# A third score buffer, four score banks and a vector-matrix product in half rows, in the recurrence of a two-block model

## The chip, the cores and the metric

The kernel runs on one core of a Trainium2 chip as one launch. The metric is device time in microseconds (us) of that launch; the time shown for a version is a median over runs. The engines are named as the profile names them: PE (TensorE, matrix products), PEld (its weight loads), DVE (VectorE), ACT (ScalarE), POOL (GpSimd), SP (SyncE, which issues most DMAs).

## The reference, cut to what matters

Two blocks act on 512 positions of width 1024. The first one mixes with a gated recurrence in two directions over 256 context and 512 sequence positions, 8 heads of 64, and is modulated by six vectors that come from a vector-matrix product:

```python
mod = jax.nn.silu(c) @ ada_w[l] + ada_b[l]            # 1024 -> 6 * 1024
sh1, sc1, g1, sh2, sc2, g2 = jnp.split(mod, 6)
...
def step(S, inp):                                     # one position of the recurrence
    r_t, w_t, kk_t, b_t, v_t, k_t = inp
    sa = jnp.einsum("bhvk,bhk->bhv", S, kk_t)
    S = S * w_t - sa * b_t + v_t * k_t                # (axes left out)
    return S, jnp.einsum("bhvk,bhk->bhv", S, r_t)
...
x = x + g1 * out_x                                    # then a gated conv FFN with sh2, sc2, g2
```

The first third of `mod` (sh1, sc1) is needed before the recurrence. The other two thirds (g1, sh2, sc2, g2) are needed only after it: "the second part of the modulation" of this text. Block two (another mixer, an FFN) follows and is not touched.

## The kernel before, in words

**Stages.** The recurrence is worked in chunks of 64 positions: 4 context chunks, 8 sequence chunks, in both directions (d = 0 and 1). The 8 heads are taken two at a time, which gives four stages, j = 0 to 3, written by `stage`. A stage has 12 steps g, each for both directions. A step solves for its chunk with a precomputed 64x64 inverse and updates the state `S0`:

- `pr` = A V + KR S0, copied by ACT to `R`; `pu` = XT R, copied by ACT to `U` with a minus; `p3` = kt0 V + S0 + kt1 U, copied by ACT to `S0` with a scale; in the 8 sequence chunks also `py` = three products, copied by ACT to `Y`.

Each product is one call of `mmh`, two 64x64 matmuls for the two heads of the pair. The trace calls the PSUM tiles of all of them `c`, R and U together `RU`, and S0 `S`; the lists of the instruction order give the tiles numbers.

**Scores and keys.** Every second step `pair` makes the inputs of two chunks for each direction: the scores `psc` (PE), which DVE copies through a mask into `AS` (L730), and the transposed keys `pkt` (PE), which ACT copies to `kbt` (L188). `AS` has two buffers for each direction and `psc`, `pkt`, `pv`, `pg`, `py` share two PSUM banks (tag `sc`). Four more banks hold the steps: `C1[d]` for pr, pu and py, `C2[d]` for p3. The last two of the eight belong to the preparation.

**Preparation.** `prep(j)` computes what stage j needs: decays, keys, and by `inverse` the matrices `XT`. It begins on DVE with a transpose `U<-AK` (L662), goes on with 31 pairs of dependent DVE operations (`tmp<-U,X`, L670, and `X<-X,tmp`, L671), then two transposes `F<-X` (L673, L674), matmuls `pt` (L690) and `po`, and ACT copies into `XT` (for stage 1 the trace calls it `zx`). `AK` has one buffer, so the inverse of j + 1 begins only after the `pt` matmuls of j have read it. Preparation 1 begins before the recurrence; 2 and 3 run beside stages 0 and 1 and into 2.

**The second part of the modulation.** `ada12` (L525 on) makes 32 output columns of 128: for each, a DMA of 512 KB into a buffer `w`, and one DVE multiply with a running sum (L540) of 128x1024 elements by silu(c). It takes part in the work list only from stage 2 on, because its buffers come from a pool that opens after preparation 3.

**After the stages.** `gn(j)` normalises the output of stage j over 12 small steps beside stage j + 1; for j = 3 there is no later stage, and beside it run the first products of the output projection, `px` (L169 to L171), on inputs 0 to 6, which `rwkv` emits behind the loop, and the splits of its weights on ACT and DVE (`whi` L181, `wlo` L182). The last input, `ahi[7]`/`alo[7]`, comes out of `gn(3)`; behind it `out_proj1` begins (L910).

**What sets the order.** The Python code only emits instructions with a priority number; a scheduler builds one fixed queue for each engine from data dependences, priorities and a model of durations. Each engine then works its queue strictly in order: an instruction that waits holds up everything behind it. Step g of a stage has priority base + 200 g; `gn` 300 later, preparation about 110 later (`PG`, `PF`, `PK`).

Of the kernel before, what the change touches and what calls it, by code (L numbers as in the profile page):

```python
# [122 lines left out]
class K:  # L123
# [8 lines left out]
    PK, PG, PF = 200, 300, (110, 105, 118, 0)  # L132
# [393 lines left out]
    def ada12(self):  # L526

        nc, wp = self.nc, self.wp
        tags = [("w", self.wbufs), ("whi", self.wsbufs), ("wlo", self.wsbufs)]
        cb, sb = (wp.tile([P, 1024], F32, tag=tags[i][0], name="cb", bufs=tags[i][1]) for i in (1, 2))  # L530
        nc.sync.dma_start(out=cb, in_=self.A["cb"])
        nc.scalar.activation(out=sb, in_=cb, func=AF.Tanh, scale=0.5)
        nc.vector.tensor_scalar(out=sb, in0=sb, scalar1=0.5, scalar2=0.5, op0=ALU.mult, op1=ALU.add)
        nc.vector.tensor_tensor(out=cb, in0=sb, in1=cb, op=ALU.mult)
        acc = wp.tile([P, 32], F32, name="adacc")
        for n in range(32):
            yield
            w, t = (wp.tile([P, 1024], F32, tag=tags[i][0], name="adaw", bufs=tags[i][1]) for i in (0, 2))
            nc.sync.dma_start(out=w, in_=self.A["adat"][n])
            nc.vector.scalar_tensor_tensor(out=t, in0=w, scalar=1.0, in1=cb, op0=ALU.mult, op1=ALU.mult, accum_out=acc[:, n:n + 1])  # L540
            if n in (7, 23, 31):
                a = 0 if n == 7 else 8 if n == 23 else 24
                nc.vector.tensor_tensor(out=self.mod[:, 16 + a:17 + n, 0], in0=acc[:, a:n + 1], in1=self.v("ada_b", 16 + a, n + 1 - a), op=ALU.add)
# [91 lines left out]
    def mmh(self, out, lt, rt, start=True, stop=True):  # L635

        for h in range(2):
            hs = slice(64 * h, 64 * h + 64)
            self.nc.tensor.matmul(out[hs], lt[hs], rt[hs], start=start, stop=stop)
# [63 lines left out]
    def stage(self, j, S, todo, rb, gn):  # L703
# [10 lines left out]
        def pair(i, d):  # L714
# [19 lines left out]
            kt = r2.tile([P, 2, 2, 64], F32, tag="kbt", name="kbt", bufs=4)  # L734
# [4 lines left out]
        for g in range(12):  # L739
            at = base + self.PK * g  # L740
            with self.prio(at):
                if g % 2 == 0:
                    for d in range(2):
                        pair(g // 2, d)
                for d in range(2):
                    c = chunk(d, g)
                    A, kt, KR, x = cells.pop((d, c))
                    V, S0 = vt[:, c, :], self.S0[d]
                    R, U = (self.RU[d][g % 2][:, i, :] for i in range(2))
                    pr, pu, py = (self.C1[d][:, i * 64:i * 64 + 64] for i in range(3))  # L750
                    p3 = self.C2[d][:, 0:64]
                    self.mmh(pr, A[:, 0:64], V, True, g == 0)
                    if g:
                        self.mmh(pr, KR[:, 0:64], S0, False, True)
                    nc.scalar.activation(out=R, in_=pr, func=AF.Copy)
                    if g < 11:
                        self.mmh(p3, kt[:, 0], V, True, False)
                        if g:
                            self.mmh(p3, id2, S0, False, False)
                    self.mmh(pu, XT[:, 12 * d + c, :], R)  # L760
                    nc.scalar.activation(out=U, in_=pu, func=AF.Copy, scale=-1.0)
                    if x:
                        self.mmh(py, A[:, 64:P], V, True, False)
                        self.mmh(py, KR[:, 64:P], S0, False, False)
                    if g < 11:
                        self.mmh(p3, kt[:, 1], U, False, True)
                        nc.scalar.activation(out=S0, in_=p3, func=AF.Copy, scale=S["PC"][d][:, c:c + 1])
                    if x:
                        self.mmh(py, A[:, P:192], U, False, True)
# [9 lines left out]
    def gn(self, j, Y, bo, vt):  # L779
# [8 lines left out]
        pv = self.ps2.tile([P, 8, 64], F32, tag="sc", name="pv", bufs=2)  # L788
# [7 lines left out]
        def gate():  # L796
            pg = self.ps2.tile([P, NX], F32, tag="sc", name="pg", bufs=2)
# [26 lines left out]
        py = self.ps2.tile([P, 8, 64], F32, tag="sc", name="py", bufs=2)  # L824
# [569 lines left out]
```

## Time and profile before

| | |
|---|---|
| median of 3 runs (1590.5 to 1594.64) | 1591.91 us |
| the profiled execution: its own time, and its span | 1588.74 us, 1586.9 us |
| busy: PE | 1503.9 us (95%) |
| busy: DVE | 1000.5 us (63%) |
| busy: ACT | 631.3 us (40%) |
| busy: POOL | 124.0 us (8%) |
| the L540 multiplies | 32, 1235 ns each |
| the DMAs of `adaw` from `in_adat` | 32 of 512 KB, median 4.5 us to landing |

A page of the profile gives each engine's busy time. Small matmuls are pipelined, so a PE that counts as 90% busy in the recurrence can be one that mostly waits for ACT between two products: what bounds that stretch is read from the order of time and from the waits, not from the share.

### The profile page before, as it was taken

What the parts mean: (1) busy time and instruction counts of PE and PEld (TensorE: products, weight loads), DVE (VectorE), ACT (ScalarE), POOL (GpSimd) and SP (SyncE); (2) the same over time, 40 slices, a digit from 0 to 9 for tenths busy, and PEclk for the clock granted to TensorE, in tenths of its full rate; (3) what the DMA queues carried; (4) which work ended last, traced back from release to release, by engine and by line L of the source; (5) the groups of instructions that cost most, each with busy time, mean ns of one, the idle gap of its engine ahead of it and who ended that gap; (6) DMA issues with size and microseconds to landing.
All of it is one profiled execution on the core that took longest, in us unless ns stands there. A gap on an engine that the chain in (4) does not pass through costs nothing. (4 is left out here: it accounts for less than half of the span.)

```text
span 1586.9 us, 28915 instructions
## 1 busy us (share of the span) xinstructions
PE 1503.9 (95%) x12062; PEld 1235.6 (78%) x12062; DVE 1000.5 (63%) x1689; ACT 631.3 (40%) x1258; POOL 124.0 (8%) x141
## 2 busy tenths in 40 slices
PE   4999999989898999999999997999999999999998
PEld 2877788777787898888888876887777888888886
DVE  3446767685867679888863438588965555554221
ACT  3524345555453444333332325345544333333122
POOL 1111001021110000000000014122200000000000
PEclk9999999898979999999999998999999999999999
DMA  9243321010058613233333332211112322233221
GB/s 340 87 156 103 101 94 56 3 46 4 14 190 263 217 53 107 93 102 98 93 94 89 96 100 65 79 54 54 40 54 93 93 93 93 94 94 106 93 92 54
DMA packets 62180, 152.83 MB, mean 96 GB/s; under 512 B 12641, under 2 KB 14433, under 8 KB 62049
## 3 DMA queue, kind: packets, MB, share of 16 engines
q1 hardware_dynamic: 58016, 143.95, 28.5%
q10 hardware_dynamic: 4032, 7.04, 1.3%
q8 instruction: 94, 1.54, 0.4%
q14 instruction: 38, 0.30, 0.1%
HBM read 143.10 MB, written 7.86 MB: 95 GB/s over the span
## 5 line engine op out<-in xcount | busy, mean ns | idle before, releaser
L181 ACT ACTIVATE whi<-w 128x1024 fp32r<-128x1024 f32 (+2 forms) x220 | 208.8, 950 | 450.7 <-PE pm L170 333.4
L182 DVE TENSOR_TENSOR wlo<-w,whi 128x1024 fp32r<-128x1024 f32 (+2 forms) x212 | 230.2, 1088 | 199.3 <-ACT whi L181 194.1
L169 PE MATMUL pm<-ahi,whi 128*128 128x512 f32 (+1 forms) x624 | 237.2, 380 | 3.0 <-DVE sh L1077 2.6
L170 PE MATMUL pm<-alo,whi 128*128 128x512 f32 (+1 forms) x624 | 235.4, 377 | 0.0
L171 PE MATMUL pm<-ahi,wlo 128*128 128x512 f32 (+1 forms) x624 | 234.6, 376 | 0.0
L170 PE MATMUL pm<-al,whi 128*128 128x512 f32 x352 | 139.7, 397 | 0.0
L169 PE MATMUL pm<-ah,whi 128*128 128x512 f32 x352 | 139.2, 395 | 0.0
L171 PE MATMUL pm<-ah,wlo 128*128 128x512 f32 x352 | 139.2, 395 | 0.0
L169 PEld LDWEIGHTS pm<-ahi,whi 128*128 128x128 f32 x624 | 117.9, 189 | 24.5 <-ACT sh L1092 3.0
L171 PEld LDWEIGHTS pm<-ahi,wlo 128*128 128x128 f32 x624 | 118.0, 189 | 20.9 <-issue 0.7
L170 PEld LDWEIGHTS pm<-alo,whi 128*128 128x128 f32 x624 | 118.1, 189 | 20.3 <-issue 0.7
L950 DVE SCALAR_TENSOR_TENSOR cv<-pm,vec,cv 128x441 f32<-128x441 f32 (+2 forms) x176 | 121.0, 693 | 4.1
L171 PEld LDWEIGHTS pm<-ah,wlo 128*128 128x128 f32 x352 | 66.2, 188 | 16.1 <-issue 0.2
L170 PEld LDWEIGHTS pm<-al,whi 128*128 128x128 f32 x352 | 66.2, 188 | 16.1 <-issue 0.2
L169 PEld LDWEIGHTS pm<-ah,whi 128*128 128x128 f32 x352 | 66.2, 188 | 16.0
L169 PE MATMUL pm<-hhi,whi 128*128 128x512 f32 x176 | 71.3, 405 | 0.2 <-ACT whi L181 0.2
L171 PE MATMUL pm<-hhi,wlo 128*128 128x512 f32 x176 | 70.1, 399 | 1.2 <-DVE wlo L182 1.2
L170 PE MATMUL pm<-hlo,whi 128*128 128x512 f32 x176 | 70.2, 399 | 0.0
L169 PE MATMUL pd<-whi,gh 128*128 128x512 f32 x176 | 69.5, 395 | 0.0
L169 PE MATMUL pm<-hh,whi 128*128 128x512 f32 x176 | 69.3, 394 | 0.0
L170 PE MATMUL pm<-hl,whi 128*128 128x512 f32 x176 | 69.3, 394 | 0.0
L171 PE MATMUL pm<-hh,wlo 128*128 128x512 f32 x176 | 69.3, 394 | 0.0
(397 smaller groups left out, 3098.5 us busy)
## 6 DMA issues: line engine op xcount, KB each, us to landing
w<-in_fup SPq DMA_DIRECT2D x44, 512.0 KB, 3.7
adaw<-in_adat SPq DMA_DIRECT2D x32, 512.0 KB, 4.5
w<-in_win SPq DMA_DIRECT2D x44, 256.0 KB, 2.9
w<-in_wg SPq DMA_DIRECT2D x22, 512.0 KB, 3.7
w<-in_wu SPq DMA_DIRECT2D x22, 512.0 KB, 3.6
w<-in_wd SPq DMA_DIRECT2D x22, 512.0 KB, 3.7
w<-in_win SPq DMA_DIRECT2D x18, 512.0 KB, 3.7
w<-in_wout SPq DMA_DIRECT2D x16, 512.0 KB, 3.8
```

The lines of the kernel that those rows point to most:

```text
L169: nc.tensor.matmul(out, lh, rh, start=(first and i == 0), stop=False)
L170: nc.tensor.matmul(out, lh, rl, start=False, stop=False)
L171: nc.tensor.matmul(out, ll, rh, start=False, stop=(last and i == n - 1))
L181: self.nc.scalar.activation(out=hi, in_=src, func=AF.Copy)
L182: (eng or self.nc.vector).tensor_tensor(out=lo, in0=src, in1=hi.bitcast(F32), op=ALU.subtract)
L950: nc.vector.scalar_tensor_tensor(out=o, in0=p[:, ro[0] + dr:ro[1] + dr, co[0] + dc:co[1] + dc], scalar=w(i), in1=o, op0=ALU.mult, op1=ALU.add)
```

## The change

- `AS` gets three buffers for each direction, the tag `sc` four PSUM banks, `kbt` six buffers. The banks come from `C2`, which goes: p3 moves into the bank `C1[d]`, beside pr, pu and py.
- In a step the products of one bank now keep the order in which they are written (an order token on each matmul), and that order is new: pu before p3, and all three products of p3 in front of py.
- `ada12` takes half rows of 512 in three buffers of its own from the start, so a work list `mods` of 64 halves can run from stage 0 on: 16 in each stage, at priority +150 (`PM`). Its sums get a second column and one more addition.
- `gn` takes one more small step: between the power on POOL and the multiply on DVE.

```diff
-    PK, PG, PF = 200, 300, (110, 105, 118, 0)
+    PK, PG, PM, PF = 200, 300, 150, (110, 105, 118, 0)
...
-        self.AS = [[st(f"AS{d}{i}", [2, 192]) for i in range(2)] for d in range(2)]
+        self.AS = [[st(f"AS{d}{i}", [2, 192]) for i in range(3)] for d in range(2)]
...
-        self.C2 = [self.ps2.tile([P, 512], F32, name=f"c2{d}") for d in range(2)]
+        self.mods = self.ada12()
...
-                todo = chain(self.splits(), self.ada12(), self.first())
+                todo = chain(self.splits(), self.first())
...
-        for _ in todo:
+        for _ in chain(self.mods, todo):
             pass
...
+        nc, r2 = self.nc, self.r2
+        H = NX
+        adw = lambda: r2.tile([P, H], F32, tag="adw", name="adw", bufs=3)
...
         for n in range(32):
-            yield
-            w, t = (wp.tile([P, 1024], F32, tag=tags[i][0], name="adaw", bufs=tags[i][1]) for i in (0, 2))
-            nc.sync.dma_start(out=w, in_=self.A["adat"][n])
-            nc.vector.scalar_tensor_tensor(out=t, in0=w, scalar=1.0, in1=cb, op0=ALU.mult, op1=ALU.mult, accum_out=acc[:, n:n + 1])
+            for i in range(2):
+                yield
+                w = adw()
+                nc.sync.dma_start(out=w, in_=self.A["adat"][n][:, i * H:i * H + H])
+                nc.vector.scalar_tensor_tensor(out=w, in0=w, scalar=1.0, in1=cb[:, i], op0=ALU.mult, op1=ALU.mult, accum_out=acc[:, n, i:i + 1])
...
-            A = self.AS[d][i % 2]
+            A = self.AS[d][i % 3]
...
-            ps = self.ps2.tile([P, 2, N], F32, tag="sc", name="psc", bufs=2)
-            pt = self.ps2.tile([P, 2, 2, 64], F32, tag="sc", name="pkt", bufs=2)
+            ps = self.ps2.tile([P, 2, N], F32, tag="sc", name="psc", bufs=4)
+            pt = self.ps2.tile([P, 2, 2, 64], F32, tag="sc", name="pkt", bufs=4)
...
-                    pr, pu, py = (self.C1[d][:, i * 64:i * 64 + 64] for i in range(3))
-                    p3 = self.C2[d][:, 0:64]
...
+                    pr, pu, py, p3 = (self.C1[d][:, i * 64:i * 64 + 64] for i in range(4))
+
+                    mm = lambda *a: self.mmh(*a, order=f"c1{d}")
+                    mm(pr, A[:, 0:64], V, True, g == 0)
                     if g:
-                        self.mmh(pr, KR[:, 0:64], S0, False, True)
+                        mm(pr, KR[:, 0:64], S0, False, True)
                     nc.scalar.activation(out=R, in_=pr, func=AF.Copy)
+                    mm(pu, XT[:, 12 * d + c, :], R)
+                    nc.scalar.activation(out=U, in_=pu, func=AF.Copy, scale=-1.0)
                     if g < 11:
-                        self.mmh(p3, kt[:, 0], V, True, False)
+                        mm(p3, kt[:, 0], V, True, False)
                         if g:
-                            self.mmh(p3, id2, S0, False, False)
-                    self.mmh(pu, XT[:, 12 * d + c, :], R)
-                    nc.scalar.activation(out=U, in_=pu, func=AF.Copy, scale=-1.0)
+                            mm(p3, id2, S0, False, False)
+                        mm(p3, kt[:, 1], U, False, True)
                     if x:
...
-                        self.mmh(p3, kt[:, 1], U, False, True)
                         nc.scalar.activation(out=S0, in_=p3, func=AF.Copy, scale=S["PC"][d][:, c:c + 1])
...
+            with self.prio(at + self.PM):
+                for _ in range(1 + (g % 3 == 0)):
+                    next(self.mods, None)
...
         nc.gpsimd.tensor_tensor(out=rs, in0=v, in1=self.mhalf[:, 0:8], op=ALU.pow)
+        yield
         nc.vector.tensor_tensor(out=yc, in0=yc, in1=wide(rs), op=ALU.mult)
```

The queues of the engines move at three places. The first is DVE's queue in the middle of the first inverse that runs beside the recurrence. `tmp` and `X` are the dependent pair, `AS` a score copy, `KB` and `b` belong to the next preparation. Before:

```order
L671 TENSOR_TENSOR X<-X,tmp 128x18x14
L615 TENSOR_TENSOR KB_2360<-b_2790,sg 128x12x64
L670 TENSOR_TENSOR tmp<-U,X 128x255
L621 TENSOR_TENSOR KR_2362<-rt,cs 128x8x64
L671 TENSOR_TENSOR X<-X,tmp 128x17x15
L730 COPY_PREDICATED AS_2367<-cst,psc 128x384
```

The same place now, where `adw` is a half row of the modulation:

```order
L678 TENSOR_TENSOR tmp<-U,X 128x255
L544 SCALAR_TENSOR_TENSOR adw,adacc<-adw,cb 128x512
L679 TENSOR_TENSOR X<-X,tmp 128x17x15
L544 SCALAR_TENSOR_TENSOR adw,adacc<-adw,cb 128x512
L678 TENSOR_TENSOR tmp<-U,X 128x256
L544 SCALAR_TENSOR_TENSOR adw,adacc<-adw,cb 128x512
L679 TENSOR_TENSOR X<-X,tmp 128x16x16
L738 COPY_PREDICATED AS_2366<-cst,psc 128x384
```

Half rows stand between the dependent operations of the inverse: 28 of the 64 between its transposes U and F, 7 from there to the next U, 29 inside the second inverse, none behind it.

The second place is PE's queue where the `pt` matmuls of that first inverse stand. Before, steps of stage 0 (`c_2375` to `c_2378`) still lie on both sides of it:

```order
L639 MATMUL c_2375<-S_2373,KR_86 64x64 x2
L639 MATMUL c_2377<-vt,kbt 64x64
L690 MATMUL pt<-F_2520,AK 32x32 x24
L639 MATMUL c_2377<-vt,kbt 64x64
L639 MATMUL c_2377<-S_2373,cst 64x64 x2
L639 MATMUL c_2375<-RU_2370,XT_83 64x64 x2
```

Now stage 0 is over there, and what stands in front of it are scores and keys of stage 1 (`KR_1648`, `KB_1646`):

```order
L645 MATMUL psc<-KR_1648,KB_1646 64x128 x2
L645 MATMUL psc<-KR_1648,KB_1646 64x64 x2
L645 MATMUL pkt<-cst,KB_1646 64x64 x5
L698 MATMUL pt<-F_2539,AK 32x32 x24
L645 MATMUL pkt<-cst,KB_1646 64x64 x3
L645 MATMUL pa<-KR_2362,KB_2360 64x64 x11
L698 MATMUL pt<-F_2539,AK 32x32 x24
```

The steps of stage 1 follow only behind `po`; their scores are up to three pairs ahead. (In the same way the second inverse ends when all three pairs of stage 2 that fit are scored, and the third one after the first pair of stage 3.)

The third place is PE's queue in one sequence step of stage 3, one direction's bank first (`c_2375` and, for p3, `c_2377`):

```order
L639 MATMUL c_2375<-RU_2369,XT_83 64x64 x2
L639 MATMUL c_2376<-vt,AS_2367 64x64
L639 MATMUL c_2376<-S_2374,KR_87 64x64 x2
L639 MATMUL c_2378<-vt,kbt 64x64 x2
L639 MATMUL c_2378<-S_2374,cst 64x64
L639 MATMUL c_2375<-vt,AS_2365 64x64 x2
L639 MATMUL c_2375<-S_2373,KR_86 64x64 x2
L639 MATMUL c_2377<-RU_2369,kbt 64x64 x2
L639 MATMUL c_2375<-RU_2369,AS_2365 64x64 x2
```

Now, with one bank for each direction (`c_2377`, `c_2378`) and scores of the pair after between the products:

```order
L645 MATMUL c_2377<-RU_2371,XT_83 64x64 x2
L645 MATMUL c_2378<-vt,AS_2369 64x64
L645 MATMUL c_2378<-S_2376,KR_87 64x64 x2
L645 MATMUL psc<-KR_86,KB_84 64x128
L645 MATMUL psc<-KR_86,KB_84 64x64 x2
L645 MATMUL c_2377<-vt,kbt 64x64 x2
L645 MATMUL c_2377<-S_2375,cst 64x64 x2
L645 MATMUL c_2377<-RU_2371,kbt 64x64 x2
L645 MATMUL c_2377<-vt,AS_2366 64x64 x2
L645 MATMUL c_2377<-S_2375,KR_86 64x64 x2
L645 MATMUL c_2378<-RU_2373,XT_83 64x64 x2
L645 MATMUL psc<-KR_86,KB_84 64x128 x2
```

Between U (which `c<-RU,XT` feeds) and the copy of the state there now stand five products of the bank where three stood. Some of the `px` products (14 of 42) also move from behind the last step to between the last steps of stage 3.

## Rows read from the trace of the kernel before

**Rows 1.** Busy time by stretch (start:end and length, then engines, PEclk, DMA, GB/s).

```profile
261.00:324.00 63.00, 59.16 (x1396) 50.91 (x1392) 46.95 (x99) 35.80 (x124) 6.09 (x14) 0.92 0.07 23
324.00:398.00 74.00, 67.78 (x1478) 57.37 (x1476) 52.91 (x107) 38.41 (x129) 11.74 (x15) 0.86 0.04 10
398.00:462.00 64.00, 56.96 (x1334) 51.29 (x1334) 46.95 (x104) 30.38 (x114) 6.11 (x8) 0.84 0.23 76
462.00:517.00 55.00, 46.98 (x1114) 40.16 (x1110) 42.08 (x76) 22.44 (x101) 4.79 (x4) 1.00 0.80 252
```

**Rows 2.** Order of time, DVE: transposes that open (U) and close (F) each inverse.

```profile
297.44 1.98 DVE L674 STREAM_TRANSPOSE F<-X 128x1024 f32<-128x1024 f32 x1
...
322.70 1.95 DVE L662 STREAM_TRANSPOSE U<-AK 128x1024 f32<-128x1024 f32 x1 [1.84 <-POOL AK L659]
...
367.83 1.90 DVE L674 STREAM_TRANSPOSE F<-X 128x1024 f32<-128x1024 f32 x1
...
396.35 1.96 DVE L662 STREAM_TRANSPOSE U<-AK 128x1024 f32<-128x1024 f32 x1 [0.89 <-POOL AK L659]
...
433.45 1.95 DVE L674 STREAM_TRANSPOSE F<-X 128x1024 f32<-128x1024 f32 x1
```

**Rows 3.** Order of time, ACT: last copies into the inverse of stage 1.

```profile
307.04 1.96 ACT L188 ACTIVATE zx<-po 32x384 f32<-32x384 f32 x4 [1.24 <-PE po L698]
```

**Rows 4.** Order of time, DVE: an inverse's operations with and without work between.

```profile
274.57 0.40 DVE L670 TENSOR_TENSOR tmp<-U,X 128x247 f32<-128x247 f32 x1
274.90 0.95 DVE L611 SCALAR_TENSOR_TENSOR b<-ta,kk 128x768 f32<-128x768 f32 x1
275.77 0.41 DVE L671 TENSOR_TENSOR X<-X,tmp 128x247 f32<-128x247 f32 x1
...
282.37 0.42 DVE L670 TENSOR_TENSOR tmp<-U,X 128x255 f32<-128x255 f32 x1
282.83 0.42 DVE L671 TENSOR_TENSOR X<-X,tmp 128x255 f32<-128x255 f32 x1
```

**Rows 5.** Groups of DVE, 261 to 517 us (count | busy, mean ns | idle before).

```profile
L540 DVE SCALAR_TENSOR_TENSOR adaw<-adaw,cb 128x1024 f32<-128x1024 f32 x32 | 39.4, 1235 | 11.3 <-DMA adaw<-in_adat 11.1
L730 DVE COPY_PREDICATED AS<-cst,psc 128x384 f32<-128x384 int32 x32 | 18.6, 580 | 29.5 <-PE psc L639 29.3
...
L827 DVE SCALAR_TENSOR_TENSOR zx<-py,vec,zx 128x512 f32<-128x512 f32 x3 | 2.2, 746 | 0.0
```

**Rows 6.** Waits, 261 to 517 us (total us, times, longest).

```profile
DVE AS L730 <- PE psc L639: 34.5, 13, 9.6
...
DVE yc L822 <- POOL grs L821: 4.9, 3, 1.8
```

**Rows 7.** Order of time, a step of stage 3: PE.

```profile
502.54 0.28 PE L639 MATMUL c<-RU,kbt 64*64 64x64 f32 x4
...
505.62 0.28 PE L639 MATMUL c<-S,KR 64*64 64x64 f32 x4
505.74 0.28 PE L639 MATMUL c<-RU,kbt 64*64 64x64 f32 x4
...
513.48 0.45 PE L639 MATMUL c<-vt,AS 64*64 64x64 f32 x6 [0.24 <-ACT Y L188]
...
516.53 0.33 PE L639 MATMUL c<-vt,AS 64*64 64x64 f32 x4 [0.32 <-ACT RU L761]
```

**Rows 8.** Order of time, the same step: ACT.

```profile
505.18 0.22 ACT L761 ACTIVATE RU<-c 128x64 f32<-128x64 f32 x1 [0.43 <-PE c L639]
...
506.13 0.32 ACT L767 ACTIVATE S<-c,pc 128x64 f32<-128x64 f32 x1 [0.50 <-PE c L639]
...
517.93 0.21 ACT L188 ACTIVATE Y<-c 128x64 f32<-128x64 f32 x1
```

**Rows 9.** Order of time, DVE behind stage 3.

```profile
519.20 0.68 DVE L806 TENSOR_TENSOR ys<-Y 128x512 f32<-128x512 f32 x1
...
534.62 1.41 DVE L910 SCALAR_TENSOR_TENSOR zx<-px,mod,xin 128x512 f32<-128x512 f32 x2 [0.82 <-PE px L171]
```

More of the change, by code (lines that the diff above doesn't have):

```diff
@@ L526, in ada12 @@
     def ada12(self):
[L528 to L534, printed above, removed]
@@ L535, in ada12 @@
-        acc = wp.tile([P, 32], F32, name="adacc")
-        for n in range(32):
-            yield
-            w, t = (wp.tile([P, 1024], F32, tag=tags[i][0], name="adaw", bufs=tags[i][1]) for i in (0, 2))
-            nc.sync.dma_start(out=w, in_=self.A["adat"][n])
-            nc.vector.scalar_tensor_tensor(out=t, in0=w, scalar=1.0, in1=cb, op0=ALU.mult, op1=ALU.mult, accum_out=acc[:, n:n + 1])
+        nc, r2 = self.nc, self.r2
+        H = NX
+        adw = lambda: r2.tile([P, H], F32, tag="adw", name="adw", bufs=3)
@@ new lines, in ada12 @@
+        cb = r2.tile([P, 2, H], F32, name="cb")
+        acc = r2.tile([P, 32, 2], F32, name="adacc")
+        nc.sync.dma_start(out=cb, in_=self.A["cb"].rearrange("p (a b) -> p a b", b=H))
+        for i in range(2):
+            sb = adw()
+            nc.scalar.activation(out=sb, in_=cb[:, i], func=AF.Tanh, scale=0.5)
+            nc.vector.tensor_scalar(out=sb, in0=sb, scalar1=0.5, scalar2=0.5, op0=ALU.mult, op1=ALU.add)
+            nc.vector.tensor_tensor(out=cb[:, i], in0=sb, in1=cb[:, i], op=ALU.mult)
@@ L541, in ada12 @@
+        for n in range(32):
+            for i in range(2):
+                yield
+                w = adw()
+                nc.sync.dma_start(out=w, in_=self.A["adat"][n][:, i * H:i * H + H])
+                nc.vector.scalar_tensor_tensor(out=w, in0=w, scalar=1.0, in1=cb[:, i], op0=ALU.mult, op1=ALU.mult, accum_out=acc[:, n, i:i + 1])
             if n in (7, 23, 31):
                 a = 0 if n == 7 else 8 if n == 23 else 24
-                nc.vector.tensor_tensor(out=self.mod[:, 16 + a:17 + n, 0], in0=acc[:, a:n + 1], in1=self.v("ada_b", 16 + a, n + 1 - a), op=ALU.add)
+                m = self.mod[:, 16 + a:17 + n, 0]
+                nc.vector.tensor_tensor(out=m, in0=acc[:, a:n + 1, 0], in1=acc[:, a:n + 1, 1], op=ALU.add)
+                nc.vector.tensor_tensor(out=m, in0=m, in1=self.v("ada_b", 16 + a, n + 1 - a), op=ALU.add)
@@ L633, in prep, with mmh @@
         yield from self.inverse(j)
-    def mmh(self, out, lt, rt, start=True, stop=True):
+    def mmh(self, out, lt, rt, start=True, stop=True, order=None):
         for h in range(2):
             hs = slice(64 * h, 64 * h + 64)
-            self.nc.tensor.matmul(out[hs], lt[hs], rt[hs], start=start, stop=stop)
+            m = self.nc.tensor.matmul(out[hs], lt[hs], rt[hs], start=start, stop=stop)
+            if order:
+                self.tc.stamp_issue_order_token(m.ins, order)
     @contextmanager
@@ L733, in pair @@
                     self.mmh(pt[:, c, i], kb[:, c0 + c, i ^ d], id2)
-            kt = r2.tile([P, 2, 2, 64], F32, tag="kbt", name="kbt", bufs=4)
+            kt = r2.tile([P, 2, 2, 64], F32, tag="kbt", name="kbt", bufs=6)
             self.copy(nc.scalar, kt, pt)
@@ L749, in stage @@
                     R, U = (self.RU[d][g % 2][:, i, :] for i in range(2))
-                    pr, pu, py = (self.C1[d][:, i * 64:i * 64 + 64] for i in range(3))
-                    p3 = self.C2[d][:, 0:64]
-                    self.mmh(pr, A[:, 0:64], V, True, g == 0)
+                    pr, pu, py, p3 = (self.C1[d][:, i * 64:i * 64 + 64] for i in range(4))
+                    mm = lambda *a: self.mmh(*a, order=f"c1{d}")
+                    mm(pr, A[:, 0:64], V, True, g == 0)
                     if g:
-                        self.mmh(pr, KR[:, 0:64], S0, False, True)
+                        mm(pr, KR[:, 0:64], S0, False, True)
                     nc.scalar.activation(out=R, in_=pr, func=AF.Copy)
+                    mm(pu, XT[:, 12 * d + c, :], R)
+                    nc.scalar.activation(out=U, in_=pu, func=AF.Copy, scale=-1.0)
                     if g < 11:
-                        self.mmh(p3, kt[:, 0], V, True, False)
+                        mm(p3, kt[:, 0], V, True, False)
                         if g:
-                            self.mmh(p3, id2, S0, False, False)
-                    self.mmh(pu, XT[:, 12 * d + c, :], R)
-                    nc.scalar.activation(out=U, in_=pu, func=AF.Copy, scale=-1.0)
+                            mm(p3, id2, S0, False, False)
+                        mm(p3, kt[:, 1], U, False, True)
                     if x:
-                        self.mmh(py, A[:, 64:P], V, True, False)
-                        self.mmh(py, KR[:, 64:P], S0, False, False)
+                        mm(py, A[:, 64:P], V, True, False)
+                        mm(py, KR[:, 64:P], S0, False, False)
                     if g < 11:
-                        self.mmh(p3, kt[:, 1], U, False, True)
                         nc.scalar.activation(out=S0, in_=p3, func=AF.Copy, scale=S["PC"][d][:, c:c + 1])
                     if x:
-                        self.mmh(py, A[:, P:192], U, False, True)
+                        mm(py, A[:, P:192], U, False, True)
                         self.copy(nc.scalar, Y[d][:, c - 4, :], py)
@@ L787, in gn @@
         nc.gpsimd.tensor_tensor(out=bv, in0=bv, in1=wide(bo), op=ALU.mult)
-        pv = self.ps2.tile([P, 8, 64], F32, tag="sc", name="pv", bufs=2)
+        pv = self.ps2.tile([P, 8, 64], F32, tag="sc", name="pv", bufs=4)
         for i in range(8):
@@ L796, in gate @@
         def gate():
-            pg = self.ps2.tile([P, NX], F32, tag="sc", name="pg", bufs=2)
+            pg = self.ps2.tile([P, NX], F32, tag="sc", name="pg", bufs=4)
             nc.tensor.matmul(pg, gup, self.sg, start=True, stop=True)
@@ L821, in gn @@
         nc.gpsimd.tensor_tensor(out=rs, in0=v, in1=self.mhalf[:, 0:8], op=ALU.pow)
+        yield
         nc.vector.tensor_tensor(out=yc, in0=yc, in1=wide(rs), op=ALU.mult)
         yield
-        py = self.ps2.tile([P, 8, 64], F32, tag="sc", name="py", bufs=2)
+        py = self.ps2.tile([P, 8, 64], F32, tag="sc", name="py", bufs=4)
         for i in range(8):
```

## The prediction

> **What bounds the kernel now.** I first read the busy time by stretch: stages 0 to 3 take 63, 74, 64 and 55 us, and DVE is busy for 47, 53, 47 and 42 of them, so it idles for some 54 us in the first three [rows 1]. All that the change moves lies there or in the 17 us behind; from 535 us on nothing moves. Next the waits: DVE stood 34.5 us at score copies whose matmuls had not come, once for 9.6 us [rows 6]. An engine works its queue in order, so whatever lay behind such a copy stood too, the next preparation included. Then the order of time, for the preparations: the inverses close at 297.4, 367.8 and 433.5, while the stages that need them begin near 324, 398 and 462 [rows 1, 2]. Inverse 1 still needs its last matmuls and copies, until 309.0, which is 11.6 us behind its F [rows 2, 3]; add the same to the others and each is ready 15 to 19 us before its stage. So the preparations do not bound the kernel now. The steps do: 12 steps in 55 us are 4.6 us each in stage 3, and one step without score work between is the 3.2 us from 502.54 to 505.74 [rows 1, 7]. The missing 1.4 us a step are scores and the stop for their copies.
>
> **The change part by part.**
>
> *The multiplies that go.* 32 of 1235 ns, 39.4 us, and 11.3 us of idle time before them leave DVE between 451 and 517 us [rows 5]. PE did not wait for them directly; they held up score copies, which the third score buffer cures anyway.
>
> *The 64 halves that come.* A half has no row. From below the nearest is the multiply of 512 from PSUM, 746 ns; from above half of 1235 plus half of the idle time, about 800 ns [rows 5]. Beside the dependent pairs of an inverse it costs less. tmp to X is 0.46 us apart with nothing between and 1.20 with a 0.95 us operation between: that operation cost 0.74, or 0.21 less than it lasts [rows 4]. So a half costs about 0.55 us there, and at most 0.8 where it finds its DMA late. The queue now holds 28 halves inside inverse 1, 7 up to the next U, and 29 inside inverse 2. This lengthens the preparations, which have the 15 to 19 us of slack and no more.
>
> *Followed through.* Inverse 1: 28 x 0.55 = 15, the silu in halves (four operations, 2), seven more score copies in its span at up to 0.58 without a wait [rows 5] (3), late DMAs 2: F at 297.4 + 22 = 320. From F to the next U it was 25 us, with the 9.6 us stop in it; with PE out of work there I take 22: U at 342. Inverse 2 took 45.1; plus 29 x 0.55 = 16, no more wait of the yc multiply for POOL (1.6 each [rows 6]): 60, F at 402. To U it was 28.5, now 24: 426. Inverse 3 took 37.1; without three of the score copies and without yc's wait 33: F at 459 or 460, 26 us later than before. The inverse for stage 3 is ready 11 us on, at 470.
>
> So the preparation takes over as the bound. Stage 1 begins near 331 instead of 324, stage 2 near 413 instead of 398, stage 3 at 470 instead of 462, however early the scores are. Bounds: with every half in time that DVE idled away (54 us, more than 64 x 0.75 = 48) stage 3 could start at 455; with each half at 0.8 us, no gain between the inverses and the stages' own work in the way, at 485. I take 470, since the halves stand inside the dense inverses, not where DVE idles.
>
> *The steps.* With its scores a pair ahead, a step no longer stops for them. But p3 in the bank of pr, pu and py adds waits. PE's first product of the next step, which writes other columns, waited 0.24 us for the copy of Y, and one behind pu 0.32 us for the copy to U [rows 7]: by these rows a write waits for any read of its bank. Three consequences. The first two products of p3, which ran while R was copied, now stand behind U: 2 x 0.12 us [rows 7]. The copy of S0 waits for all five products, and the last py must wait until S0 is copied; then Y, then the next pr. Y began 0.21 us behind S0's start, now S0's 0.32, a hop and a product come between, 0.76 (the hop from product to copy: 505.74 to 506.13, 0.39 [rows 7, 8]). That makes a sequence step 0.23 + 0.55 = 0.8 longer than 3.2: 4.0 us, with the score matmuls now inside its waits. A context step has no py: I take 2.8. Stage 3: 4 x 2.8 + 8 x 4.0 = 43 us. Bounds: 36 us, if steps stay at 3.2 (8 x 3.2 + 4 x 2.6), and 50, if score matmuls, which cost PE 0.12 us a call, come on top of 4.0 for 0.6 a step and 14 early px in stage 3 cost their time.
>
> The Trainium skill, "PSUM — Partial Sum Buffer", section "PSUM bank collisions raise a hardware error", says to guard PSUM with semaphores by bank and quadrant, not by address. Both waits in this trace agree. By address alone p3 could start under R's copy and py under S0's, a step would stay near 3.2, and stage 3 would take the 36 us.
>
> *The end.* Stage 3 ends at 470 + 43 = 513 instead of 518.1 (Y at 517.93 [rows 8]): -5. Behind it gn(3) runs 16.5 us from there to the first L910 at 534.62. Its first operation on DVE waited till 519.20 for the split of a weight [rows 9], and three more splits lay between its operations (the queue shows them). They now precede the last score copies, so 1.0 and some 2.5 us go: -3.5. 28 px are still there to run beside it. The extra `yield` in gn puts other work before yc's multiply, which took away 4.9 us of DVE waits in all [rows 6]; that is counted above. The third buffer's six memsets and the six kbt buffers lie beside projection matmuls: nothing, or 1 us where DVE is late.
>
> Sum: -5 - 3.5 = -8.5. The profiled execution took 1588.74 us, 3.2 under the median of 1591.91; by the same difference 1580.2 there is 1583.4 as a median. I predict 1583.
>
> **The rivals.**
>
> *The halves cost the preparation nothing.* For it: DVE's 54 idle us, 29.5 of which stood before score copies [rows 5]. Against it: halves are fixed in the queue inside the inverses. Stage 3 then starts at 455, the lower bound above, and is over 43 us later, at 498 instead of 518: -20, and -3.5 for the tail, so 1568.
>
> *The bound is only exchanged.* Stage 3 starts at 474 to 478 and what its steps gain is used up: end at 518 to 520, less the tail's 3: within 2 us, 1591. For it: the slack was 15 to 19 us, the halves add 48 us of DVE work in front of the third inverse and 26 us by my sum. Against it: the stops at score copies go from between the inverses.
>
> *Slower: preparation and one bank.* If halves wait for their DMAs (three buffers of 256 KB; before, 11.1 of 39 us of multiplies were waited for [rows 5]) and the F to U stretches don't shorten, F of inverse 3 comes at 475 and stage 3 starts at 486. With steps at 43 us it ends at 529, 11 us late, less 3.5: +8, 1600. It decides from a start of stage 3 beyond 478.
>
> *The scores don't get ahead.* Score copies still stand in DVE's queue behind transposes of 1.9 us. Then steps stay near 4.6 and start late: 470 + 55, +7 - 3.5, 1595. The queue of PE speaks against it: it has three pairs of stage 1 scored before `pt`.
>
> **How the numbers follow.** About 5 us (0.3%) is what a measurement here can tell from no change. Forecast, 1576 to 1590 by its own bounds of step and start: 0.45. Free halves: 0.20. Exchanged bound: 0.17. Slower by preparation and bank: 0.13. Scores not ahead: 0.05. Faster by over 0.3%: 0.20 and four fifths of the forecast's 0.45, and a little of the exchange, 0.58. Within: the rest of the forecast, most of the exchange and some of the last two, 0.24. Slower: 0.18. The range for 8 in 10 leaves out the outer parts of the first and third rival: 1567 to 1599.
>
> **What would show it.** Right: F of the third inverse near 460 (450 to 470), stage 3 from about 470 to 513, steps of 4 us with PE waiting for copies of Y and S0, no DVE wait over 2 us at score copies, PE empty behind stage 0 until about 331, gn(3) in 13 us. Wrong in the halves: F of the third inverse before 450, or behind 475. Wrong in the steps: sequence steps of 3.3 us, or over 4.5. Wrong altogether: anything over 2 us that moves behind 535 us or before 261 us.

## The result, and the profile after

The changed kernel takes 1600.25 us (median of 6 runs, 1596.06 to 1605.25) against 1590.5 us for the kernel before (6 runs beside them): a ratio of 1.0057, with a 95% interval of 1.0037 to 1.0077. It is slower by some 10 us, clear of the 5 us that a measurement here can tell. Forecast was 1583, 8.5 us faster.

The profiled execution took 1604.72 us with a span of 1602.9, 16.0 more than before. (It is the second longest of the six; the medians lie 9.75 apart.) I read it in the same order as before. First DVE's transposes that open (U) and close (F) the inverses:

```profile
264.11 1.96 DVE L670 STREAM_TRANSPOSE U<-AK 128x1024 f32<-128x1024 f32 x1 [0.47 <-POOL AK L667]
...
329.46 1.91 DVE L682 STREAM_TRANSPOSE F<-X 128x1024 f32<-128x1024 f32 x1
...
355.72 1.95 DVE L670 STREAM_TRANSPOSE U<-AK 128x1024 f32<-128x1024 f32 x1 [0.97 <-POOL AK L667]
...
422.09 1.90 DVE L682 STREAM_TRANSPOSE F<-X 128x1024 f32<-128x1024 f32 x1
...
449.84 1.96 DVE L670 STREAM_TRANSPOSE U<-AK 128x1024 f32<-128x1024 f32 x1 [2.01 <-POOL AK L667]
...
478.26 1.99 DVE L682 STREAM_TRANSPOSE F<-X 128x1024 f32<-128x1024 f32 x1
```

Before, the last F came at 433.45 [rows 2]. The recurrence opens 3.8 us later in this execution (U at 264.11; before it was 260.28). Where these 3.8 us come from is not shown: halves_behind (below), which has all the buffers and banks of the change, opens at 259.31, and the granted clock from 180 to 220 us is 0.83 here and 0.91 in before and in halves_behind. Counted from that first U, the third inverse closes after 214.2 us instead of 173.2: **41 us later**. The second inverse is later still (158.0 after U, against 107.6); the third, which has no half in it, took 28.4 us instead of 37.1 and gave 8.7 back. Next what stands between the dependent operations, in DVE's order of time:

```profile
303.34 0.68 DVE L544 SCALAR_TENSOR_TENSOR adw<-adw,cb 128x512 f32<-128x512 f32 x1
303.94 0.08 DVE L544 DVE_READ_ACCUMULATOR adw<-adw,cb 128x1 f32 x1
303.94 0.41 DVE L678 TENSOR_TENSOR tmp<-U,X 128x247 f32<-128x247 f32 x1
304.27 0.69 DVE L544 SCALAR_TENSOR_TENSOR adw<-adw,cb 128x512 f32<-128x512 f32 x1
304.88 0.08 DVE L544 DVE_READ_ACCUMULATOR adw<-adw,cb 128x1 f32 x1
304.88 0.41 DVE L679 TENSOR_TENSOR X<-X,tmp 128x247 f32<-128x247 f32 x1
```

From tmp to X is 0.94 us with a half between; a pair of nearly this size (255 for 247) stands 0.46 apart alone [rows 4]. Then the groups of DVE from 255 to 535 us:

```profile
L544 DVE SCALAR_TENSOR_TENSOR adw<-adw,cb 128x512 f32<-128x512 f32 x64 | 45.6, 714 | 7.8 <-DMA adw<-in_adat 7.4
```

And the stretches in which PE ran out of work (columns as in [rows 1]), with the waits of PE and DVE from 200 to 560 us (total, times, longest):

```profile
321.00:345.00 24.00, 20.65 (x482) 18.01 (x484) 17.73 (x41) 10.78 (x27) 6.61 (x7) 0.74 0.45 137
...
400.00:437.00 37.00, 22.04 (x484) 18.96 (x484) 23.68 (x63) 10.56 (x25) 6.41 (x7) 0.65 0.26 76
...
485.00:496.00 11.00, 10.26 (x215) 8.43 (x213) 6.38 (x10) 8.91 (x21) 3.18 (x2) 0.63 0.53 183
496.00:540.00 44.00, 42.79 (x992) 36.10 (x991) 11.79 (x19) 21.98 (x94) 2.03 (x2) 1.00 0.13 42
```

```profile
PE pt L698 <- DVE F L682: 15.6, 2, 13.5
...
DVE AS L738 <- PE psc L645: 24.0, 12, 4.8
```

The first of these two lines in the kernel before:

```profile
PE pt L690 <- DVE F L674: 3.6, 3, 1.4
```

The steps of stages 0 and 1 are over at some 321 and 400 us. PE then works off what is left of scores and preparation and comes to `pt`, which waits for F: behind stage 1 for 13.5 us. The steps of stages 1 and 2 go on only with their first copies of U, on ACT:

```profile
341.29 0.45 ACT L766 ACTIVATE RU<-c 128x64 f32<-128x64 f32 x2
...
433.14 0.45 ACT L766 ACTIVATE RU<-c 128x64 f32<-128x64 f32 x2
```

The granted clock from 400 to 437 us is 0.65, so it was at the lower of its two levels for most of that stretch. What was slack before is now the bound: the preparation.

Last, the entry into stage 3 on ACT and its last copy, and the end on DVE:

```profile
486.42 1.99 ACT L188 ACTIVATE XT<-po 32x384 f32<-32x384 f32 x4 [1.26 <-PE po L706]
488.42 2.71 ACT L181 ACTIVATE ahi<-zx 128x512 fp32r<-128x512 f32 x5
491.03 1.99 ACT L181 ACTIVATE whi<-w 128x1024 fp32r<-128x1024 f32 x2
492.93 0.61 ACT L181 ACTIVATE ahi<-zx 128x512 fp32r<-128x512 f32 x1
493.56 0.22 ACT L188 ACTIVATE Y<-c 128x64 f32<-128x64 f32 x1
493.69 0.22 ACT L766 ACTIVATE RU<-c 128x64 f32<-128x64 f32 x1
...
541.07 0.22 ACT L188 ACTIVATE Y<-c 128x64 f32<-128x64 f32 x1 [0.93 <-PE c L645]
```

```profile
541.32 1.15 DVE L818 TENSOR_TENSOR ys<-Y 128x512 f32<-128x512 f32 x1 [8.31 <-ACT Y L188]
...
554.93 1.41 DVE L923 SCALAR_TENSOR_TENSOR zx<-px,mod,xin 128x512 f32<-128x512 f32 x2 [0.82 <-PE px L171]
```

In the kernel before, the first copy of a U of stage 3 is this one:

```profile
463.55 0.44 ACT L761 ACTIVATE RU<-c 128x64 f32<-128x64 f32 x2 [0.37 <-PE c L639]
```

So the 20.3 us by which the end of gn(3) is later (554.93 against 534.62 [rows 9]) are: +3.8 at the start, +41.0 to F, -14.7 of slack used up (from F to the first U of stage 3 it is 15.4 us, 478.3 to 493.7, where it was 30.1, 433.45 to 463.55), -7.0 in stage 3 (493.69 to the last Y at 541.07, against 463.55 to 517.93), -2.8 behind it. Later 4.3 us come back (last section). The third inverse is barely the last thing that stage 3 waits for: its XT is copied at 488.4. Stage 2, whose first U came 20 us later than forecast because of the second inverse, has its last U copied at 484.8, only 3.6 us earlier.

### The profile page after: what moved, and what is told of

The parts are those of the page before. It is cut to its first block, busy times and chain, and to the rows that moved or that the text cites. A ratio compares the mean times of both kernels' runs of the same rounds, so it can differ in the third digit from the quotient of the medians.

```text
span 1602.9 us, 29044 instructions
## 1 busy us (share of the span) xinstructions
PE 1507.3 (94%) x12062; PEld 1238.1 (77%) x12062; DVE 997.0 (62%) x1760; ACT 630.9 (39%) x1259; POOL 124.8 (8%) x141
## 5 line engine op out<-in xcount | busy, mean ns | idle before, releaser
L171 PE MATMUL pd<-whi,gl 128*128 128x512 f32 x176 | 69.5, 395 | 0.0
L170 PE MATMUL pd<-wlo,gh 128*128 128x512 f32 x176 | 69.5, 395 | 0.0
```

What stands on the lines that cost most here:

```text
L170: nc.tensor.matmul(out, lh, rl, start=False, stop=False)
L171: nc.tensor.matmul(out, ll, rh, start=False, stop=(last and i == n - 1))
```

## The experiments

Ratios are to the kernel before as it ran beside each kernel, with 95% intervals. "U to F" runs from the first U to the close of the third inverse in the profiled execution; the last column is the end of gn(3) there (the first operation of `out_proj1` on DVE, L910 in before, another line number elsewhere), counted from the same U. These two columns come from one execution each, and that need not be a middle one: in one_bank_only it is 8 us above the median, in the change and halves_only 5 above, in halves_between 5 below.

| kernel | median us | ratio | U to F | U to L910 or its like |
|---|---|---|---|---|
| before | 1589.93 to 1591.35 | | 173.2 | 274.3 |
| the change | 1600.25 | 1.0057 [1.0037, 1.0077] | 214.2 | 290.8 |
| late_rows | 1590.57 | 1.0009 [0.9993, 1.0026] | 173.2 | 275.3 |
| halves_only | 1599.66 | 1.0072 [1.0049, 1.0094] | 208.2 | 287.8 |
| one_bank_only | 1591.97 | 1.0024 [0.9999, 1.0049] | 176.1 | 281.4 |
| third_buffer_only | 1593.59 | 1.0027 [1.0010, 1.0044] | 171.2 | 273.6 |
| no_rows | 1577.79 | 0.9927 [0.9901, 0.9952] | 172.7 | 267.7 |
| halves_behind | 1590.71 | 1.0011 [0.9995, 1.0027] | 171.5 | 279.2 |
| halves_between | 1583.26 | 0.9961 [0.9943, 0.9980] | 175.2 | 265.4 |
| halves_between_old_banks | 1586.72 | 0.9977 [0.9960, 0.9994] | 180.0 | 277.8 |
| splits_later | 1600.29 | 1.0063 [1.0041, 1.0086] | 215.8 | 291.4 |
| between_splits_later | 1576.59 | 0.9910 [0.9891, 0.9929] | 176.4 | 264.1 |
| between_16 | 1585.98 | 0.9963 [0.9947, 0.9980] | 189.4 | 274.3 |
| own_buffers | 1590.02 | 0.9995 [0.9978, 1.0012] | 165.9 | 276.3 |

**The parts of the change, one at a time.** late_rows is the changed kernel with `ada12` of before:

```diff
-        self.mods = self.ada12()
...
-                todo = chain(self.splits(), self.first())
+                todo = chain(self.splits(), self.ada12(), self.first())
```

> The changed kernel with one part undone: the 32 multiplies of the modulation are full rows behind preparation 3 again, as before the change; third score buffer, four score banks and p3 in one bank stay. Theory A (the halves inside the inverses delay the preparation, which sets when stage 3 starts): F of the third inverse comes 57 x 0.55 = 31 us earlier than in the changed kernel, at about 445 us, stage 3 starts near 460, and the total is 15 to 25 us below the changed kernel, 1575 to 1585 us. Rival B (the one bank and the new order of products make the steps long, and the halves only fill idle time): within 5 us of the changed kernel, 1595 to 1605 us.

The way is A's: 10 us back, and F closes 41 us earlier, counted from U:

```profile
263.46 1.95 DVE L663 STREAM_TRANSPOSE U<-AK 128x1024 f32<-128x1024 f32 x1 [0.47 <-POOL AK L660]
...
436.70 1.96 DVE L675 STREAM_TRANSPOSE F<-X 128x1024 f32<-128x1024 f32 x1
```

The size is not: the time lies between the two ranges, level with the kernel before and not 5 to 15 us below it.

halves_only gives the kernel before the half rows of the change with their list `mods`, and nothing else (the diff shows the list's place):

```diff
+            with self.prio(at + self.PM):
+                for _ in range(1 + (g % 3 == 0)):
+                    next(self.mods, None)
```

> The kernel before with one part of the change: the 64 half rows in all four stages; two score buffers, two score banks and p3 in its own bank stay. Theory A: the halves lengthen inverses 1 and 2 by 31 us less what DVE idled there, stage 3 starts 20 to 30 us late and is some 5 us shorter without the multiplies; total 1605 to 1615 us, slower than the changed kernel. Rival B (halves fill idle time): 1580 to 1592 us.

Slower by 10 us, 5 less than A said and as slow as the whole change. So the halves alone make the loss, with either set of score buffers and banks.

The two kernels show one thing more. From the first U of stage 3 to the end of its last Y it is 54.6 us in before and 54.3 in late_rows, which has the scores ahead and the one bank; it is 47.5 in halves_only, which has neither, and 47.6 in the change. The kernels below go the same way: 50.6 and 51.2 us in the two others that have no multiply in stage 3 (no_rows, splits_later), 52.6 to 58.6 in all that have some there. So what made stage 3 shorter in the change is mainly that the full rows left it; that the new buffers and banks did is not shown.

one_bank_only is the kernel before with the new order of products, its order tokens, and

```diff
-                    pr, pu, py = (self.C1[d][:, i * 64:i * 64 + 64] for i in range(3))
-                    p3 = self.C2[d][:, 0:64]
+                    pr, pu, py, p3 = (self.C1[d][:, i * 64:i * 64 + 64] for i in range(4))
```

> The kernel before with one part of the change: p3 in the bank of pr, pu and py, with the order tokens and the new order of the products; two score buffers, two score banks and late full rows stay. Theory A: steps get up to 0.8 us longer where they don't wait for scores anyway, 0 to 20 us in all; total 1592 to 1610 us. Rival B: the bank is the whole loss, 10 us, and more without the scores ahead: 1600 us or above, and late_rows is slow too. Rival C: the bank costs nothing, 1588 to 1593 us.

Within the noise, 2 us above; its own runs scatter from 1584.65 to 1602.25, so between A's low end and C nothing is decided; B, as the whole loss, falls.

third_buffer_only is the kernel before with

```diff
-        ... for i in range(2)] for d in range(2)]
+        ... for i in range(3)] for d in range(2)]
-            kt = r2.tile(..., tag="kbt", name="kbt", bufs=4)
+            kt = r2.tile(..., tag="kbt", name="kbt", bufs=6)
```

> The kernel before with one part of the change: three score buffers and six key buffers; two score banks, p3 in its own bank and late full rows stay. If the stop of DVE at score copies is a matter of buffers of the copies (a pair further ahead), 5 to 10 us faster, 1580 to 1586 us. If the two banks that scores, keys and gn share are the limit, the score matmuls come no earlier: within 3 us, 1588 to 1593 us.

The score copies still wait 29.2 us (34.5 before [rows 6]), and the time is no lower (0.1 to 0.4% higher by the interval). The Trainium skill, "Perfetto Trace Analysis", section "Optimization Strategy", says that a gap that repeats on the engine that should be saturated can mean too few buffers. Here the gaps were on DVE, which is not the saturated engine of the steps, and a buffer more gave nothing.

**Without the multiplies, and in other places.** no_rows takes the load and the multiply out of the changed kernel:

```diff
-                w = adw()
-                nc.sync.dma_start(out=w, in_=self.A["adat"][n][:, i * H:i * H + H])
-                nc.vector.scalar_tensor_tensor(out=w, in0=w, scalar=1.0, ...)
+                pass
```

> The changed kernel without the multiplies and their loads: the second part of the modulation is left out (its sums are zero). It prices the 64 halves where the change put them, and shows what scores ahead and one bank give when nothing is in their way. Theory A (halves in the inverses cost 41 us at F of the third inverse, 30 of them beyond what the preparation has to spare, and full rows behind it cost stage 3 10 us): F at 437 us, stage 3 44 us long and over at about 508 us, 1577 to 1583 us, so 18 to 23 below the changed kernel and 8 to 13 below late_rows. Rival B (the loss is in the steps and banks): 1590 us or more.

1577.8 and F after 172.7 us, as A said; stage 3 is over at 516.8 and not at 508, the gain lies partly behind it. (Stage 3 starts no earlier after U than before.) Its waits, from 261 to 518 us, hold the surprise:

```profile
L737 DVE COPY_PREDICATED AS<-cst,psc 128x384 f32<-128x384 int32 (+1 forms) x48 | 23.5, 490 | 47.6 <-PE psc L644 47.4
```

DVE stands **longer** at score copies than before (47.4 us against 34.5), in a kernel that is 12 us faster. The sum of that wait does not set the time.

halves_behind gives each half its factor 1 from a column that is written behind F, so that none can be queued ahead of it:

```diff
+            nc.vector.tensor_scalar(out=self.one, in0=F2[:, 0, 0:1], scalar1=0.0, scalar2=1.0, op0=ALU.mult, op1=ALU.add)
...
-                nc.vector.scalar_tensor_tensor(out=w, in0=w, scalar=1.0, ...)
+                nc.vector.scalar_tensor_tensor(out=w, in0=w, scalar=self.one, ...)
```

> The changed kernel with all 64 halves behind the third inverse: each multiply takes its factor 1 from a column that is written behind F of that inverse. Same instructions, other place. Theory A: F of the third inverse at 437 us instead of 478, stage 3 about 54 us with the halves in it, total 1586 to 1592 us. Rival B (it is the number of halves and their loads that cost, not the place): 1596 to 1603 us. Rival C (half rows let score copies through where full rows of 1.2 us stop them): 1580 to 1586 us.

A again: same 64 halves, 10 us less. B and C fall. The halves now run until 535 us and hold up gn(3): from the end of stage 3 to its L910 it takes 23 us, DVE 15.69 of them busy (the last 1.8 us are a wait for a load of `xin`):

```profile
515.50:538.50 23.00, 11.29 (x100) 8.19 (x99) 15.69 (x39) 2.17 (x4) 2.68 (x2) 0.69 0.52 163
```

halves_between writes such a column behind each F and releases 12, 12 and 40 halves:

```diff
+            with self.prio(self.tc.cur_priority + self.PM):
+                for _ in range((0, 12, 12, 0)[j]):
+                    next(self.mods, None)
```

> The changed kernel with 12 halves held behind F of the first inverse, 12 behind F of the second and 40 behind F of the third, so that none stands inside an inverse. Theory A: between F and the next U DVE idles 10 to 14 us, which takes 12 halves of 0.72 us; F of the third inverse at 437 to 445 us, stage 3 4 us shorter than with all 64 behind: 1582 to 1588 us. Rival D (they hold up the operations that prepare the next inverse by their full 0.72 us): F of the third at 455 us, 1590 to 1597 us.

Within A's range, and the first kernel with all of the work in it that beats both the kernel before and the change. F moves by 4 us only (175.2 after U against 171.5). But the gain is not in stage 3, which still takes 53 us; it lies behind it, where gn(3) is free of halves:

```profile
462.30:515.30 53.00, 48.40 (x1107) 40.00 (x1105) 32.34 (x81) 23.86 (x102) 4.51 (x3) 1.00 0.51 167
515.30:529.00 13.70, 12.06 (x117) 9.08 (x116) 6.46 (x12) 2.17 (x4) 2.68 (x2) 1.00 0.19 58
```

halves_between_old_banks is halves_only with those two edits (the factor from a column behind each F; 12, 12 and 40).

> The same placement of the halves (12, 12, 40) with the two score buffers, two score banks and p3 in a bank of its own of the kernel before. Theory A, with third buffer and one bank worth nothing together: within 3 us of halves_between, 1582 to 1588 us. If scores ahead pay once the halves are out of the inverses, it is 5 us or more behind halves_between; if the one bank costs, as much ahead of it.

It is 3.5 us behind by the medians, between the two cases, and the intervals of the two ratios overlap. Their runs, 12 each beside one another, have means 2.8 us apart, 0.1 to 5.5 by a 95% interval: third buffer, four banks and one bank together are worth a few us at most once the halves are out of the inverses, and whether they are worth anything is hardly decided. (The two profiled executions are further apart than that, 10 us, and so are the rows of the table.)

between_16 has `(0, 16, 16, 0)[j]` and 32 behind the third.

> halves_between with 16, 16 and 32 half rows instead of 12, 12 and 40. If DVE's idle time between F and the next U takes 16 as well as 12, stage 3 and gn lose 8 halves: 1580 to 1583 us. If that gap is full at 12, each further half moves the next U by 0.7 us and F of the third inverse by 5 to 6: 1584 to 1588 us.

The second case: the third inverse closes 189.4 us after the first U instead of 175.2, so eight more halves cost 14 us of preparation there, 12.7 of them in the two stretches from F to U (34.0 and 34.5 us instead of 28.8 and 27.1). That the room between F and U ends near 12 is read from these two executions, whose times lie 10 us apart. The total is 3 us above halves_between by the medians; the intervals overlap.

**The splits at the entry of stage 3.** splits_later is the changed kernel, and between_splits_later is halves_between, with the five `ahi` splits held until step 1 of stage 3 has given a U:

```diff
+            if j == 3 and g == 1:
+                nc.gpsimd.tensor_scalar(out=self.oneS, in0=U[:, 0:1], scalar1=0.0, scalar2=1.0, op0=ALU.mult, op1=ALU.add)
...
-            self.split(self.ahi[k], self.alo[k], self.zx[k])
+            self.nc.scalar.activation(out=self.ahi[k], in_=self.zx[k], func=AF.Copy, scale=self.oneS)
```

> The changed kernel, halves where the change put them, with the five ACT splits of the inputs of the output projection held until a step of stage 3 has run. In the changed kernel they stand in ACT's queue between the last copies into the third inverse (488.4 us) and the first copy of a U of stage 3 (493.7). Theory E (they are the other part of the late start of stage 3): first U copy 3 to 5 us behind those copies less than now, total 1595 to 1597 us. Rival: the two weight splits and scores that stand there too keep stage 3 from starting earlier, or the splits come back in stage 3: 1599 to 1602 us.

The first U comes 1 us behind the copies into XT instead of 5.3:

```profile
486.82 1.99 ACT L188 ACTIVATE XT<-po 32x384 f32<-32x384 f32 x4 [1.14 <-PE po L707]
488.82 0.63 ACT L181 ACTIVATE ahi<-zx 128x512 fp32r<-128x512 f32 x1
489.47 0.22 ACT L188 ACTIVATE Y<-c 128x64 f32<-128x64 f32 x1
489.79 0.22 ACT L767 ACTIVATE RU<-c 128x64 f32<-128x64 f32 x1
```

Yet the last U of stage 3 is copied by 539.9, as in the changed kernel (540.1), and the total is the same: the rival holds, what is moved comes back in stage 3.

> halves_between (12, 12 and 40 half rows behind the F of the three inverses) with the same five ACT splits held until stage 3 runs. Theory E: the stretch in which two steps of stage 2 took 16 us gets 3 to 4 us shorter, 1579 to 1581 us. Rival: stage 2 ends earlier but the splits and px then lie in stage 3 or behind it: 1582 to 1585 us.

Here it pays: 1576.6 us, 0.9%, 14 us, faster than the kernel before, and the best kernel of this study. The gain on halves_between is more than E said by the medians (6.7 us) and less in the two profiled executions (spans of 1573.9 and 1576.4). How much of it is the splits' I leave open. ACT's queue at that place shows 3.5 us of it: from XT to the first copy of a step it is 4.6 us in halves_between (453.72 - 449.14), first below, and 1.0 in between_splits_later (451.25 - 450.21):

```profile
447.17 1.96 ACT L188 ACTIVATE XT<-po 32x384 f32<-32x384 f32 x4 [2.03 <-PE po L714]
449.14 2.71 ACT L181 ACTIVATE ahi<-zx 128x512 fp32r<-128x512 f32 x5
451.75 1.04 ACT L181 ACTIVATE whi<-w 128x1024 fp32r<-128x1024 f32 x1
452.70 0.61 ACT L181 ACTIVATE ahi<-zx 128x512 fp32r<-128x512 f32 x1
...
453.72 0.23 ACT L772 ACTIVATE RU<-c 128x64 f32<-128x64 f32 x1
```

```profile
448.23 1.97 ACT L188 ACTIVATE XT<-po 32x384 f32<-32x384 f32 x4 [2.42 <-PE po L715]
450.21 0.63 ACT L181 ACTIVATE ahi<-zx 128x512 fp32r<-128x512 f32 x1
...
451.25 0.23 ACT L773 ACTIVATE RU<-c 128x64 f32<-128x64 f32 x1
```

**The buffers of the multiplies.** own_buffers is halves_only with all halves held behind the third F by the same kind of column.

> The kernel before with only the form of the multiplies changed: 64 half rows in three buffers of their own, all behind F of the third inverse; scores, banks and steps as before. In the kernels whose multiplies have buffers of their own the part behind the first L910 (or its like) took 1040 to 1042 us, where full rows in the weight buffers gave 1045 to 1046. If the buffers are the reason, that part is 3 to 5 us shorter here too, with stage 3 as before: 1585 to 1589 us. If it came from the scores, banks or gn of the change, it is 1045 again and the total 1589 to 1593 us.

The part behind the first L910 took 1041.5 us against 1045.6 to the same last product, so the first case holds for it. It does not hold everywhere: in halves_only, whose multiplies have the same buffers, all that is behind the first L910 took 1051.8 us against 1052.3. And with the halves in it, stage 3 took 4 us more than before (58.6 against 54.6) and gn(3) 3.4 more (19.9 against 16.5), so the total is that of the kernel before.

## Why the prediction was wrong, by its steps

*The mechanism was named, the sum was not large enough.* "The preparation takes over as the bound" is what the trace shows. F of the third inverse was forecast 26 us late and came 41 us late, counted from the first U. The step that failed is "Followed through". Place by place (us):

| | before | forecast | the change | late_rows |
|---|---|---|---|---|
| first inverse, U to F | 37.2 | 59.7 | 65.3 | 43.9 |
| F to the next U | 25.3 | 22 | 26.3 | 22.5 |
| second inverse | 45.1 | 60 | 66.4 | 47.5 |
| F to the next U | 28.5 | 24 | 27.8 | 22.6 |
| third inverse | 37.1 | 33 | 28.4 | 36.8 |
| in all | 173.2 | 198.7 | 214.2 | 173.2 |

- *The halves.* The price inside an inverse was right: 0.55 us (0.92 against 0.37 from one dependent operation to the next, medians of 37 halves that found their load and of 11 pairs alone, in the first two inverses). What the sum left out are the waits beside them. In the first inverse DVE waited 4.2 us for ACT before `KB` and `b` of the next preparation, and 2.6 for scores (0.9 before). In the second it waited 5.1 us for scores (0.4 before) and 3.7 for loads of halves, which the sum had late only in the first. late_rows against the change gives 41 us for all 64, 0.64 a half.
- *The credit between the inverses.* I booked 7.5 us there, because DVE would no longer stop at score copies. These stops did go: 21.6 us of them before, 2.0 in the change. Other things took their place: seven halves in the first stretch, which I had not counted there, and in the second one wait for ACT:

```profile
435.28 0.62 DVE L190 TENSOR_SCALAR sg<-sg,cst 128x768 f32<-128x768 f32 x1 [10.42 <-ACT sg L585]
```

  The products that ACT's `sg` is made from stand in PE's queue behind `pt` and `po` of the inverse, and PE reached them only at 430.6 us. So the late inverse held up the next preparation as well. In late_rows the two stretches are 8.7 us shorter, as I had said, but the first two inverses are 9.1 longer: the stops had moved into them (9.7 us, 1.3 before). In all nothing of the credit came, in either kernel.
- *The third inverse* was shorter than forecast by 4.6 us, which went the other way.

*From F to stage 3* I took the 11 us that XT needs. It was 15.4: 10.1 until XT is copied (478.3 to 488.4) and 5.3 of splits on ACT. Before they stood in the slack; splits_later shows that without them the stage starts earlier, though nothing is won with that in the changed kernel.

*The steps* were too short in the sum, within its bounds. In stage 3 one direction's copies of R stand 4.4 us apart in the sequence steps (mean of 14, from 3.4 to 5.6; 4.0 forecast) and 3.3 in the context steps (2.8 forecast). From the first U to the last Y stage 3 took 47.6 us (43 forecast), and gn(3) behind it 13.6 (13 forecast; 16.5 before). That a step waits for its one bank is seen: ACT waits for the last product of the bank before each of these two copies of the state, one step of 4.09 us apart:

```profile
508.40 0.31 ACT L776 ACTIVATE S<-c,pc 128x64 f32<-128x64 f32 x1 [0.96 <-PE c L645]
508.61 0.22 ACT L764 ACTIVATE RU<-c 128x64 f32<-128x64 f32 x1
...
512.49 0.31 ACT L776 ACTIVATE S<-c,pc 128x64 f32<-128x64 f32 x1 [0.96 <-PE c L645]
512.70 0.21 ACT L764 ACTIVATE RU<-c 128x64 f32<-128x64 f32 x1
```

But the gain that I gave to the scores ahead went with the rows that left (stage 3 took 54.6 and 54.3 us with them, 47.5 and 47.6 without, see above), and those I had put at nothing for PE, as something that "the third score buffer cures anyway".

*Added up*, with the 3.8 us of the start taken off: against the forecast F is 15 us late, the first U of stage 3 19.9, the last Y 24.5, the first L910 25.0.

*The rivals.* "Slower: preparation and one bank", which I gave 0.13, is what happened in kind: halves waited for their loads (7.4 us) and the ways from F to U did not shorten. Its places are too early (F at 475, 478.3 measured; stage 3 from 486, 493.7 measured, to 529, 541.3 measured), and that its total of 1600 us is the measured median is luck: 4.3 us that came back later were in nobody's sum, and the profiled execution is 4.5 us above the median. Of "The scores don't get ahead" the first half came true (DVE still stood 24.0 us at score copies), the second did not: the sequence steps were 4.4 us and not 4.6.

*Points that the forecast excluded:* 3.8 us moved ahead of 261 us, which stays open, and 4.3 us behind 535 us, see below.

## What to carry to other kernels

Work that fills an engine's idle time is free only where the scheduler can't put it between the dependent operations of a chain: here the chain had some 15 us of slack, and 64 halves at 0.6 us each took that and more. Hold such work back by a data dependence on the chain's end, and give each gap only what it holds: 12 halves in each of two gaps cost the preparation 4 us, 16 cost it 18 (one execution each). A wait that goes is not yet a gain: here waits of DVE went from one place and came back in another, and in no_rows the longest of them grew while the time fell. Before you book a removed wait, look for the kernel in which it grows and the time falls.

## What was not expected

In the kernel before, FFN products run some 2% slower than in the changed kernel from 277 to 402 us behind the first L910: they follow one another every 233 ns, and every 229 in the changed kernel (mean), while just ahead of that stretch it is 227 in both. From some 340 to 420 us behind the first L910, from one and the same product to another it is 79.8 us in before, late_rows, one_bank_only and third_buffer_only, and 78.6 to 78.7 in the other kernels for which I took it, whose multiplies have buffers of their own or are left out (own_buffers among them, where nothing else is changed). Where I took the granted clock of that stretch (before, the changed kernel, late_rows, halves_only), it is 1.00. By 402 us this makes 2.5 us of the 4.3 that come back; halves_only has these 2.5 us too, and not the rest. The rotation or the addresses of the weight buffers, in which the full rows took part, would fit; neither was tried.
